# Two gate-and-up pieces of a feed-forward taken as one pair, 512 columns wide

## The chip, the cores and the metric

The kernel runs on one core of a Trainium2 chip. The metric is the device time of one execution in microseconds. Three runs of the kernel before took 752.0, 753.22 and 754.83 us; the median is 753.22.

## The reference

A trunk of two layers over 256 tokens of width 1024: dilated attention, a SwiGLU feed-forward, forgetting attention, a second feed-forward, a last norm. The change lies in the two feed-forwards:

```python
def rmsnorm(x, g):
    xf = x.astype(jnp.float32)
    y = xf * lax.rsqrt(jnp.mean(xf * xf, axis=-1, keepdims=True) + RMS_EPS) * g.astype(jnp.float32)
    return y.astype(x.dtype)

def swiglu(h, w_gu, w_down):
    gu = h @ w_gu
    g, u = gu[..., :D_FF], gu[..., D_FF:]
    return (jax.nn.silu(g) * u) @ w_down
...
        h = h + swiglu(rmsnorm(h, ffn_norm[i]), ffn_w_gu[i], ffn_w_down[i])
```

D_FF is 2816, that is 22 slices of 128.

## The kernel before

**Precision.** Every float32 operand is split into a high and a low part (`split`, L71): ScalarE copies it to the high tile, rounded (L74), VectorE subtracts that from the source into the low tile (L78). A product is then three matrix products, high by high (L197), high by low and low by high (L202), in `mm3`. With `narrow`, `mm3` issues each of the last two as two halves of the columns.

**Weights.** They are streamed through the chip once. `piece` (L85) loads 2048 columns in two transfers of 128 x 1024 into `raw` (five buffers, queue of SP) and splits each half into `wh` and `wl` (four buffers each). `order` lists all pieces in the order in which they go through these buffers; `weights(nm, i)` sees to it that the pieces up to two places behind the wanted one are issued, and hands the wanted one out. In a feed-forward the list is gu0, gu1, gu2, dn0, gu3, gu4, dn1, gu5, gu6, dn2 and so on, so that the fifth piece takes the buffer that the first gives up.

A gate-and-up piece gu*f* holds slice *f* of the gate and slice *f* of the up projection, 128 columns each, for all eight depth blocks of 128.

**The normalised rows.** `xt` holds the normalised activations, features on partitions, high and low. The first token half (t = 0, 128 tokens) is there when the feed-forward starts; the second is made during its first products by `norm_t(*hs[1], grow, xt, 1)`: a scale on VectorE (L185, `xn`), eight transposes on TensorE (L190) into two `tr` banks, and the split from there into `xt`.

**Two forms of a gate-and-up product.** `up(f)` has the weights as the stationary operand and both token halves as 256 moving columns; its result has features on partitions, as the down projection needs it. It wants both token halves. `proj_tok` (L215) has one token half of `xt` as the stationary operand and the piece's 256 columns moving; its result has tokens on partitions and must be transposed afterwards, but one token half is enough. So the first three pieces of each feed-forward, the head, go through `proj_tok`, first for the first token half, all three, with `norm_t` of the second half hooked in at the third depth block of gu2, then for the second half. After that half of a piece `gated` (L674) takes Silu on ScalarE (L677) and the product on VectorE (L678) for both halves at once; two transposes (L730) and a split into `acts` follow. Down projections (`down`) take two slices at a time: down(0) needs slices 0 and 1, down(1) slices 2 and 3.

**The pair.** `proj_pair` (L225) is there before, for value projections of both attentions. It takes two pieces that were laid out so that each holds 512 columns of half of the depth: four depth blocks per piece. Its products move 512 columns. At the last depth block of t = 1 it is narrow.

**Buffers in PSUM.** Eight banks in four tags of two: `mm`, `tr`, `sc`, `o`. The head's three pieces use two of one tag and one of another, `o, o, mm` in the first feed-forward and `mm, mm, o` in the second. down(0) takes both `sc` and both `o`, `up` one `mm` and one `tr`.

**Order.** Tile's scheduler puts the instructions of each engine in order of priority and of their place in the program; `first()` raises the priority, `tc.issue_after` ties it to an instruction. Each engine works through its own queue in that order.

Of the kernel before, what the change touches and what calls it, by code (L numbers as in the profile page):

```python
# [16 lines left out]
P = 128  # L17
D = 1024
S = 256
KT = D // P  # L20
# [4 lines left out]
NF = DFF // P  # L25
# [6 lines left out]
def trunk(ctx: ExitStack, tc: tile.TileContext, T, out):  # L32
# [14 lines left out]
    def psum(tag):  # L47
        return ps.tile([P, 512], F32, tag=tag, name=f"ps_{tag}", bufs=2)
# [88 lines left out]
    for l in range(2):  # L137
        if l == 1:
            order += [("b_in", hq * 3 + w) for hq, w in b_units]
            order += [("b_out", i) for i in range(4)]  # L140
        for f in range(NF):
            order += [(f"gu{l}", f)] + ([(f"dn{l}", f // 2 - 1)] if f % 2 == 0 and f else [])
        order += [(f"dn{l}", NJ - 1)]
    AHEAD = 2
    ready = {}
# [2 lines left out]
    def weights(nm, i, after=None, ahead=AHEAD):  # L148

        upto = order.index((nm, i)) + ahead  # L150
        while state["next"] <= min(upto, len(order) - 1):
            key = order[state["next"]]
            cuts = []
            ready[key] = piece(key, cuts)
            for cut in cuts:
                cut(after)
            state["next"] += 1
        return ready.pop((nm, i))
# [506 lines left out]
    def ffn(l, hs, xt, grow, mid):  # L665
# [3 lines left out]
        def act(f):  # L669
            if f % 2 == 0:  # L670
                acts[f // 2] = tuple(p_tile(512, F32R, f"a{y}") for y in "hl")
            return acts[f // 2], lambda y: y[:, (f % 2) * S:(f % 2 + 1) * S]
# [42 lines left out]


        dn = {}
        head = []
        for f in range(3):
            head.append((weights(f"gu{l}", f), psum((("o", "o", "mm"), ("mm", "mm", "o"))[l][f])))  # L720
            proj_tok(xt, head[f][0], head[f][1][:, :S], 0,
                     hook=(2, lambda: norm_t(*hs[1], grow, xt, 1)) if f == 2 else None)
        for f in range(3):
            o = head[f][1]
            proj_tok(xt, head[f][0], o[:, S:], 1)
            ov = o.rearrange("p (a c b) -> p a c b", a=2, c=2)
            a = gated(ov[:, :, 0, :], ov[:, :, 1, :], 2)
            tr = psum("tr")
            for t in range(2):
                nc.tensor.transpose(tr[:, t * P:(t + 1) * P], a[:, t, :], ident)  # L730
            split(*act(f), tr[:, :S])
        for f in range(2, NF):
            if f > 2:
                up(f)
            if f % 2 == 0:
                j = f // 2 - 1
                dn[j] = weights(f"dn{l}", j)
                down(j, 0, narrow=j >= LATE)
                if j < LATE:
                    down(j, 1, narrow=True)  # L740
# [271 lines left out]
def _layout(i):  # L1012

    perm, t = _constants()
    x = np.asarray(i["x"])[0]
    t["x"] = x
    x_fm = x[perm].T.reshape(KT, P, S)
    t["norms"] = np.stack([np.asarray(i["a_norm"])[0], np.asarray(i["ffn_norm"])[0], np.asarray(i["b_norm"])[0],
                           np.asarray(i["ffn_norm"])[1], np.asarray(i["final_norm"])])
    kmaj = lambda w: w.reshape(KT, P, -1).transpose(1, 0, 2)  # L1020
    a = np.asarray(i["a_w_in"])[0].reshape(KT, P, NG, 3, 4, 256)
    a = np.ascontiguousarray(a.transpose(4, 2, 3, 1, 0, 5))

    v = np.stack([a[:, 1, 2], a[:, 2, 2]], 3).reshape(4, P, 2, 2048)
    a[:, 1:, 2] = v.transpose(0, 2, 1, 3).reshape(4, 2, P, KT, 256)

    def quarters(y):

        y = np.stack([y[:, 0], y[:, 1]], 3)
        return y.reshape(-1, P, 2, 4, 512).transpose(0, 2, 1, 3, 4).reshape(-1, 2, P, KT, 256)  # L1030

    a[:2, 0, 2] = quarters(a[None, :2, 0, 2])[0]
    t["a_in"] = a.reshape(36, P, 2048)

    lead = np.concatenate([x_fm, v[0].reshape(P, KT, 512).transpose(1, 0, 2)], 2)
    t["lead0"] = np.concatenate([lead[0], np.asarray(i["a_norm"])[0].reshape(KT, P).T], 1)
    t["lead1"] = lead[1]
    t["lead"] = lead[2:].reshape(3, 2, P, -1).transpose(0, 2, 1, 3).reshape(3, P, -1)
    b = np.asarray(i["b_w_in"])[0]
    y = np.ascontiguousarray(b[:, :3 * D].reshape(KT, P, 3, 4, 256).transpose(3, 2, 1, 0, 4))  # L1040
    y[:2, 2] = quarters(y[None, :2, 2])[0]
    t["b_in"] = y.reshape(12, P, 2048)
    t["b_f_in"] = kmaj(b[:, 3 * D:]).reshape(P, KT * NH)
    t["bf"] = np.asarray(i["b_f"])[0]
    rows = lambda w: w.reshape(-1, 2, P, D).transpose(0, 2, 1, 3).reshape(-1, P, 2048)
    t["a_out"], t["b_out"] = rows(np.asarray(i["a_w_out"])[0]), rows(np.asarray(i["b_w_out"])[0])
    for l in range(2):
        g = np.asarray(i["ffn_w_gu"])[l].reshape(KT, P, 2, NF, P)
        t[f"gu{l}"] = g.transpose(3, 1, 0, 2, 4).reshape(NF, P, 2048)
        t[f"dn{l}"] = rows(np.asarray(i["ffn_w_down"])[l])  # L1050
    return {k: np.ascontiguousarray(v) for k, v in t.items()}

# [15 lines left out]
```

## Time and profile before

| | |
|---|---|
| median of three runs | 753.22 us (752.0 to 754.83) |
| the profiled execution | 753.38 us, of which the span takes 751.6 |
| instructions | 14534 |
| TensorE | 6008 products |
| head, up(3) and down(0) of the first feed-forward | 266.45 to 296.33 us of the span |
| the same in the second | 561.49 to 591.37 us |

In the profile PE is TensorE's products and PEld its weight loads, which overlap them; DVE is VectorE, ACT ScalarE, POOL GpSimd, SP the queue that issues transfers. L202 is line 202. Products are pipelined: the lengths that the timeline gives for them overlap, and what a product costs is the distance from its start to the start of the next. A wait is shown in square brackets with the work that ended it. Windows give the busy time and the instructions of each engine in a stretch that the reader chooses.

### The profile page before, as it was taken

The numbers are of one execution on the slowest core, as the hardware profiler recorded it, in microseconds if no ns is written. First come the engines' busy times: TensorE is split into PE (matmuls) and PEld (weight loads), VectorE is DVE, ScalarE is ACT, GpSimd is POOL, SyncE is SP. The second block draws the span as 40 slices with busy tenths as digits, with TensorE's granted clock in tenths as the row PEclk, the third lists the DMA queues.
The fourth block names the chain that finished last, engine by engine and source line by source line (L and its number), as shares of the span: only waits on it lengthen the run. The fifth ranks groups of instructions, "written<-read, shape, count | busy, mean of one in ns | idle before, by whom it ended". The sixth has DMA issues, their size and how long they took to land.

```text
span 751.6 us, 14534 instructions
## 1 busy us (share of the span) xinstructions
PE 742.2 (99%) x6008; PEld 683.4 (91%) x6008; DVE 498.5 (66%) x758; ACT 374.8 (50%) x620; POOL 63.8 (8%) x98
## 2 busy tenths in 40 slices
PE   9999999999999999999999999999999999999996
PEld 7998989999988799999999988999789999999995
DVE  6987987877888376454556465798766545456533
ACT  7635527347336455444445355387555444445521
POOL 0600003004003000000000004311000000000000
PEclk9999999999999999999999999999999999999999
DMA  8954553654645267656567433795336665656601
GB/s 329 303 196 170 169 169 124 204 185 136 197 152 186 85 224 236 208 176 205 186 193 255 167 128 128 236 305 183 120 102 220 226 206 174 204 188 214 206 2 56
DMA packets 39586, 138.08 MB, mean 184 GB/s; under 512 B 4544, under 2 KB 5984, under 8 KB 39520
## 3 DMA queue, kind: packets, MB, share of 16 engines
q1 hardware_dynamic: 39376, 137.06, 54.9%
q8 instruction: 47, 0.77, 0.4%
q14 instruction: 19, 0.16, 0.1%
q10 hardware_dynamic: 144, 0.10, 0.0%
HBM read 136.07 MB, written 1.07 MB: 182 GB/s over the span
## 4 chain that ended last, share of the span: by engine, by line
PE 90%; DMA 3%; issue 2%; ACT 2%; DVE 1%; SPq 0%; POOL 0%; POOLq 0%; DVEq 0%; ACTq 0%
PE ps_mm L202 31%; PE ps_mm L197 16%; PE ps_tr L202 9%; PE ps_sc L202 8%; PE ps_o L202 7%; PE ps_tr L197 5%; PE ps_sc L197 4%; PE ps_o L197 3%; PE ps_o L304 2%; PE ps_tr L293 2%; ACT wh L74 1%; DMA otl<-in_lead 1%; DMA raw<-in_b_in 1%; PE ps_sc L450 1%; PE ps_sc L835 1%
## 5 line engine op out<-in xcount | busy, mean ns | idle before, releaser
L74 ACT ACTIVATE wh<-raw 128x1024 fp32r<-128x1024 f32 x236 | 243.7, 1055 | 244.8 <-PE ps_mm L202 81.2
L78 DVE TENSOR_TENSOR wl<-raw,wh 128x1024 fp32r<-128x1024 f32 x236 | 285.5, 1230 | 86.9 <-ACT wh L74 86.7
L197 PE MATMUL ps_mm<-xt,wh 128*128 128x256 f32 x816 | 228.2, 280 | 0.6 <-DVE qk L434 0.6
L202 PE MATMUL ps_mm<-xt,wl 128*128 128x256 f32 x816 | 226.2, 277 | 0.1
L202 PE MATMUL ps_mm<-xt,wh 128*128 128x256 f32 x816 | 226.0, 277 | 0.0
L197 PEld LDWEIGHTS ps_mm<-xt,wh 128*128 128x128 f32 x816 | 153.4, 188 | 4.3 <-issue 3.3
L202 PEld LDWEIGHTS ps_mm<-xt,wl 128*128 128x128 f32 x816 | 153.5, 188 | 0.5 <-DVE wl L78 0.5
L202 PEld LDWEIGHTS ps_mm<-xt,wh 128*128 128x128 f32 x816 | 153.4, 188 | 0.0
L202 PE MATMUL ps_tr<-xt,wl 128*128 128x256 f32 x304 | 83.8, 276 | 0.0
L202 PE MATMUL ps_tr<-xt,wh 128*128 128x256 f32 x304 | 83.8, 276 | 0.0
L197 PE MATMUL ps_tr<-xt,wh 128*128 128x256 f32 x304 | 83.6, 276 | 0.0
L693 DVE TENSOR_TENSOR sa<-ps_tr,sa 128x256 f32<-128x256 f32 x38 | 16.1, 424 | 74.7 <-PE ps_tr L202 74.7
L202 PEld LDWEIGHTS ps_tr<-xt,wh 128*128 128x128 f32 x304 | 57.1, 188 | 0.0
L202 PEld LDWEIGHTS ps_tr<-xt,wl 128*128 128x128 f32 x304 | 57.1, 188 | 0.0
L197 PEld LDWEIGHTS ps_tr<-xt,wh 128*128 128x128 f32 x304 | 56.9, 188 | 0.0
L197 PE MATMUL ps_mm<-wh,xt 128*128 128x256 f32 (+1 forms) x160 | 53.0, 331 | 0.0
L202 PE MATMUL ps_mm<-wh,xt 128*128 128x256 f32 (+1 forms) x164 | 51.9, 320 | 0.0
L202 PE MATMUL ps_mm<-wl,xt 128*128 128x256 f32 (+1 forms) x164 | 51.8, 320 | 0.0
L279 POOL COPY v<-v 32x256 f32<-32x256 f32 x64 | 33.2, 518 | 180.4 <-ACT v L275 177.7
L167 POOL TENSOR_SCALAR rs<-ssq 128x1 f32<-128x1 f32 x7 | 2.2, 319 | 430.3 <-ACT junk L176 430.3
L202 PEld LDWEIGHTS ps_mm<-wl,xt 128*128 128x128 f32 x164 | 30.8, 188 | 2.6
L202 PEld LDWEIGHTS ps_mm<-wh,xt 128*128 128x128 f32 x164 | 30.5, 188 | 2.6
(218 smaller groups left out, 1140.5 us busy)
## 6 DMA issues: line engine op xcount, KB each, us to landing
raw<-in_gu SPq DMA_DIRECT2D x88, 512.0 KB, 4.5
raw<-in_a_in SPq DMA_DIRECT2D x68, 512.0 KB, 4.4
raw<-in_dn SPq DMA_DIRECT2D x44, 512.0 KB, 4.2
raw<-in_b_in SPq DMA_DIRECT2D x24, 512.0 KB, 5.0
raw<-in_a_out SPq DMA_DIRECT2D x8, 512.0 KB, 5.2
raw<-in_b_out SPq DMA_DIRECT2D x8, 512.0 KB, 5.0
bias<-sums SPq DMA_DIRECT2D x8, 384.0 KB, 6.2
grow<-in_norms SPq DMA_DIRECT2D x4, 512.0 KB, 5.1
```

What stands on the lines that cost most here:

```text
L74: a = nc.scalar.activation(view(hi), src, AF.Copy)
L78: return nc.vector.tensor_tensor(view(lo), src, view(hi).bitcast(F32), op=ALU.subtract)
L167: nc.gpsimd.tensor_scalar(m, s, rest, None, op0=ALU.add)
L197: nc.tensor.matmul(o, sh, mh, start=start, stop=False)
L202: last = nc.tensor.matmul(o[:, u], s, m[:, u], start=False, stop=end and u.stop == n)
L279: nc.gpsimd.tensor_copy(v[1 + a % 2][n:n + 32, a // 2 * S:a // 2 * S + S], by_t[a * 32:a * 32 + 32, t, g])
L293: nc.tensor.transpose(tr[:, i * P:(i + 1) * P], b, ident)
L304: nc.tensor.matmul(o[h * HD:(h + 1) * HD], v[:, c:c + HD], w(h), start=start, stop=stop)
L450: nc.tensor.matmul(scs[h][:, qb * P:qb * P + (qb + 1) * P], q[hr[h], pr, qb * P:(qb + 1) * P], k[hr[h], pr, :(qb + 1) * P], start=True, st ...
L693: nc.vector.tensor_tensor(a, u, sg, op=ALU.mult)
L835: last = nc.tensor.matmul(scs[h][:, qb * P:qb * P + (qb + 1) * P], b[0][own[h], pr, qb * P:(qb + 1) * P], b[1][own[h], pr, :(qb + 1) * P], ...
```

## The change

The first two pieces are laid out as a pair: in memory gu0 now holds the first half of the depth of slices 0 and 1, side by side, 512 columns, and gu1 the second half. The head becomes:

1. `proj_pair` with both, first token half; Silu and product of both slices for that half (`gate(0)`).
2. The third piece, first token half, with `norm_t` of the second half hooked in as before.
3. `proj_pair`, second token half; `gate(1)`.
4. The third piece, second token half.
5. The four transposes of slices 0 and 1 into one `tr` bank, and one split of 512 columns into `acts[0]`.
6. `up(3)`; then the third piece's gate, its two transposes and its split; then down(0) and the loop as before.

Before, `up(3)` came behind down(0). In the list of pieces gu3 and dn0 change places, nothing else does. The arithmetic is the same.

```diff
-            order += [(f"gu{l}", f)] + ([(f"dn{l}", f // 2 - 1)] if f % 2 == 0 and f else [])
+            order += [(f"gu{l}", f)] + ([(f"dn{l}", max(f // 2 - 1, 0))] if f == 3 or f % 2 == 0 and f > 3 else [])
...
-        head = []
-        for f in range(3):
-            head.append((weights(f"gu{l}", f), psum((("o", "o", "mm"), ("mm", "mm", "o"))[l][f])))
-            proj_tok(xt, head[f][0], head[f][1][:, :S], 0,
-                     hook=(2, lambda: norm_t(*hs[1], grow, xt, 1)) if f == 2 else None)
-        for f in range(3):
-            o = head[f][1]
-            proj_tok(xt, head[f][0], o[:, S:], 1)
-            ov = o.rearrange("p (a c b) -> p a c b", a=2, c=2)
-            a = gated(ov[:, :, 0, :], ov[:, :, 1, :], 2)
-            tr = psum("tr")
-            for t in range(2):
-                nc.tensor.transpose(tr[:, t * P:(t + 1) * P], a[:, t, :], ident)
-            split(*act(f), tr[:, :S])
+        ws = [weights(f"gu{l}", f) for f in range(2)]
+        pair = [psum(("o", "mm")[l]) for _ in range(2)]
+        rows = {}
+
+        def gate(t):
+            gu = pair[t].rearrange("p (a c b) -> p a c b", a=2, c=2)
+            rows[t] = gated(gu[:, :, 0, :], gu[:, :, 1, :], 2)
+
+        for half in range(2):
+            proj_pair(xt, ws[half], pair, half, (0,))
+        gate(0)
+        wt, o = weights(f"gu{l}", 2), psum(("mm", "o")[l])
+        proj_tok(xt, wt, o[:, :S], 0, hook=(2, lambda: norm_t(*hs[1], grow, xt, 1)))
+        for half in range(2):
+            proj_pair(xt, ws[half], pair, half, (1,))
+        gate(1)
+        proj_tok(xt, wt, o[:, S:], 1)
+        tr = psum("tr")
+        for f in range(2):
             for t in range(2):
-                nc.tensor.transpose(tr[:, t * P:(t + 1) * P], a[:, t, :], ident)
-            split(*act(f), tr[:, :S])
+                nc.tensor.transpose(tr[:, f * S + t * P:f * S + (t + 1) * P], rows[t][:, f, :], ident)
+        act(0)
+        split(acts[0], lambda y: y, tr)
+        third = act(2)
+        up(3)
+        gu = o.rearrange("p (a c b) -> p a c b", a=2, c=2)
+        a = gated(gu[:, :, 0, :], gu[:, :, 1, :], 2)
+        tr = psum("tr")
+        for t in range(2):
+            nc.tensor.transpose(tr[:, t * P:(t + 1) * P], a[:, t, :], ident)
+        split(*third, tr[:, :S])
         for f in range(2, NF):
-            if f > 2:
+            if f > 3:
                 up(f)
...
         g = np.asarray(i["ffn_w_gu"])[l].reshape(KT, P, 2, NF, P)
-        t[f"gu{l}"] = g.transpose(3, 1, 0, 2, 4).reshape(NF, P, 2048)
+        g = g.transpose(3, 1, 0, 2, 4).reshape(NF, P, KT, 256)
+        t[f"gu{l}"] = np.concatenate([quarters(g[None, :2])[0].reshape(2, P, 2048), g[2:].reshape(-1, P, 2048)])
```

What this does to the queues, in the first feed-forward. First TensorE, before, where the head's transposes stand: in the third piece's second token half (`ps_mm_3332`), each group of two for one slice (`sa_3402` and `sa_3436` are the gated slices 0 and 1).

```order
L202 MATMUL ps_mm_3332<-wh_3252,xt_3037 128x256
L730 MATMUL ps_tr_3405<-ident_216,sa_3402 128x128 x2
L197 MATMUL ps_mm_3332<-wh_3252,xt_3037 128x256
L730 MATMUL ps_tr_3439<-ident_216,sa_3436 128x128 x2
L202 MATMUL ps_mm_3332<-wl_3253,xt_3037 128x256
```

The same now, where the third piece's second half ends and `up(3)` begins (`xt` as the moving operand marks it):

```order
L202 MATMUL ps_mm<-wl,xt 128x256
L202 MATMUL ps_mm<-wh,xt 128x256
L738 MATMUL ps_tr<-ident,sa 128x128 x4
L197 MATMUL ps_mm<-xt,wh 128x256
L202 MATMUL ps_mm<-xt,wh 128x256
L202 MATMUL ps_mm<-xt,wl 128x256
```

The four stand in one group, 24 products later relative to the second gate, with `up(3)` behind them instead of down(0). Second, VectorE around the split of the normalised second half (`xt` from `ps_tr`). Before, where `wh_3287` is dn0, `wh_3322` gu3:

```order
L185 SCALAR_TENSOR_TENSOR xn_3343<-h_a_out1_3236,rs_3339,grow_2995 128x512 x2
L78 TENSOR_TENSOR wl_3288<-raw_3291,wh_3287 128x1024
L78 TENSOR_TENSOR xt_3037<-ps_tr_3346,xt_3037 128x4x128
L78 TENSOR_TENSOR xt_3037<-ps_tr_3353,xt_3037 128x4x128
L78 TENSOR_TENSOR wl_3323<-raw_3324,wh_3322 128x1024
L78 TENSOR_TENSOR wl_3323<-raw_3326,wh_3322 128x1024
L678 TENSOR_TENSOR sa_3402<-ps_o_3262,sa_3402 128x256
L678 TENSOR_TENSOR sa_3436<-ps_o_3297,sa_3436 128x256
```

Now, where `wh_3262` is gu3, `wh_3301` dn0, `wh_3421` gu4, and `sa_3298` and `sa_3383` are the gated rows of the first and second token half:

```order
L185 SCALAR_TENSOR_TENSOR xn_3322<-h_a_out1_3236,rs_3318,grow_2995 128x512 x2
L78 TENSOR_TENSOR wl_3263<-raw_3266,wh_3262 128x1024
L678 TENSOR_TENSOR sa_3298<-ps_o_3272,sa_3298 128x256
L78 TENSOR_TENSOR xt_3037<-ps_tr_3325,xt_3037 128x4x128
L78 TENSOR_TENSOR xt_3037<-ps_tr_3332,xt_3037 128x4x128
L78 TENSOR_TENSOR wl_3302<-raw_3303,wh_3301 128x1024
L78 TENSOR_TENSOR wl_3302<-raw_3305,wh_3301 128x1024
L678 TENSOR_TENSOR sa_3383<-ps_o_3273,sa_3383 128x256
L78 TENSOR_TENSOR wl_3422<-raw_3423,wh_3421 128x1024
```

The first gate's product has moved ahead of the split of `xt`, and gu3 and dn0 have changed places. ScalarE's queue shows the same: the load of Silu's table and the first gate's Silu now stand ahead of its two copies to `xt`, and the third gate's Silu stands behind `up(3)`'s. On SP's queue gu0 to gu3 go out as eight transfers in a row, then dn0's two.

## The prediction

> **What bounds the kernel now.** I read the first page, then the engines' busy time by stretches of the span (windows), then the timeline of TensorE, VectorE and ScalarE over the head of the first feed-forward. The page first:
>
> ```profile
> span 751.6 us, 14534 instructions
> PE 742.2 (99%) x6008; PEld 683.4 (91%) x6008; DVE 498.5 (66%) x758; ACT 374.8 (50%) x620; POOL 63.8 (8%) x98
> PEclk9999999999999999999999999999999999999999
> ```
>
> TensorE is busy for 742.2 of 751.6 us at the full granted clock. Of the 9.4 us without it, nearly all lies at the two ends, as the windows show (columns: length; busy us and instructions of PE, PEld, DVE, ACT, POOL; clock; DMA share; GB/s):
>
> ```profile
> 0.00:30.00 30.00, 28.45 (x162) 24.31 (x162) 23.00 (x35) 21.80 (x35) 5.13 (x14) 1.00 0.90 320
> 735.00:752.00 17.00, 9.37 (x48) 7.80 (x46) 7.34 (x17) 3.27 (x10) 1.58 (x4) 0.93 0.17 62
> 266.45:296.33 29.88, 29.82 (x234) 28.45 (x232) 19.87 (x25) 15.67 (x25) 1.80 (x2) 1.00 0.70 234
> ```
>
> The ends hold 1.55 + 7.63 = 9.2 us of it (the last row's 17.00 reaches 0.4 us past the span). The third row is the stretch that the change rewrites in the first layer: from the first product of the feed-forward to the end of its up(3). TensorE idles there for 0.06 of 29.88 us, and the second layer repeats it. So a term counts only if it shortens what TensorE itself does, or takes away what stretches it between two products; what VectorE and ScalarE do counts only where TensorE would wait for it.
>
> **The width.** The first two pieces, each in turn over a token half, fill these four stretches of 48 products of 256 columns; the fifth row is the forgetting attention's pair of pieces, 24 units of 512 columns from the same helper, with the token half as weights too and with the same two narrow splits at its end; the last is up(3), 48 products of 256 columns with wh as weights:
>
> ```profile
> 266.45:272.11 5.66, 5.66 (x50) 5.65 (x48) 5.20 (x7) 3.33 (x7) 1.80 (x2) 1.00 0.70 248
> 275.81:281.46 5.65, 5.65 (x50) 5.65 (x49) 1.48 (x2) 2.56 (x3) 0.00 (x0) 1.00 0.51 170
> 561.49:567.15 5.66, 5.66 (x50) 5.65 (x48) 5.19 (x7) 3.33 (x7) 1.81 (x2) 1.00 0.71 231
> 570.84:576.50 5.66, 5.66 (x50) 5.66 (x49) 1.48 (x2) 2.56 (x3) 0.00 (x0) 1.00 0.44 177
> 462.56:468.07 5.51, 5.51 (x28) 4.60 (x27) 2.01 (x10) 4.29 (x5) 2.91 (x1) 1.00 0.00 0
> 290.87:296.33 5.46, 5.46 (x51) 5.46 (x49) 2.36 (x2) 2.40 (x3) 0.00 (x0) 1.00 0.88 285
> ```
>
> A product of 256 columns costs 5.66/48 = 118 ns, one of 512 costs 5.51/24 = 230 ns: joining two saves 6 ns, no more. The four stretches sum to 22.63 us, four pairs at 5.51 to 22.04: **0.59 us less in both layers**. From below the bound is nothing (512 columns at twice 118); from above it is the fastest column of the table, up(3)'s, at 24 x 2 x 5.46/48 = 5.46 a pair, 0.79 us for four. I take the pair's row, because it is the same shape with the same roles.
>
> **The transposes.** Now the end of the old head, TensorE's timeline (start, length), and the eight transposes of the normalised rows for the price of a longer group:
>
> ```profile
> 272.82 1.03 PE L190 MATMUL ps_tr<-ident,xn 128*128 128x128 f32 x8
> 273.61 0.36 PE L197 MATMUL ps_mm<-wh,xt 128*128 128x256 f32 x1
> 273.81 0.28 PE L202 MATMUL ps_mm<-wl,xt 128*128 128x256 f32 x1
> ```
>
> ```profile
> 282.76 0.28 PE L202 MATMUL ps_mm<-wh,xt 128*128 128x256 f32 x1
> 283.11 0.44 PE L730 MATMUL ps_tr<-ident,sa 128*128 128x128 f32 x2
> 283.30 0.37 PE L197 MATMUL ps_mm<-wh,xt 128*128 128x256 f32 x1
> 283.50 0.38 PE L730 MATMUL ps_tr<-ident,sa 128*128 128x128 f32 x2
> 283.64 0.36 PE L202 MATMUL ps_mm<-wl,xt 128*128 128x256 f32 x1
> 283.84 0.28 PE L202 MATMUL ps_mm<-wh,xt 128*128 128x256 f32 x1
> ...
> 285.49 0.47 PE L202 MATMUL ps_sc<-wh,al 128*128 128x512 f32 x1
> 285.80 0.40 PE L197 MATMUL ps_sc<-wh,ah 128*128 128x512 f32 x1
> ...
> 286.50 0.38 PE L730 MATMUL ps_tr<-ident,sa 128*128 128x128 f32 x2
> 286.64 0.48 PE L197 MATMUL ps_sc<-wh,ah 128*128 128x512 f32 x1
> 286.96 0.40 PE L202 MATMUL ps_sc<-wl,ah 128*128 128x512 f32 x1
> ```
>
> ```profile
> 281.46:285.02 3.56, 3.50 (x31) 3.29 (x29) 2.81 (x5) 3.55 (x7) 0.00 (x0) 1.00 0.57 201
> 576.50:580.06 3.56, 3.50 (x31) 3.29 (x29) 2.81 (x5) 3.55 (x7) 0.00 (x0) 1.00 0.70 188
> ```
>
> The third piece's second half, 24 products, should take 24 x 118 ns = 2.83 us and takes 3.56 in either layer: 0.73 us go to the four transposes of the first two pieces and the wait ahead of them (the first starts 0.35 us after the product before it, not 0.12). The eight in one group cost 273.81 - 272.82, less one product, 0.87 us; so four cost 0.44. The change gives them one group with nothing to wait for: **0.73 - 0.44 = 0.29 us a layer, 0.58 in both**. Ends: the old wait comes back too (0.23 of the 0.29 are gone), or the group goes in at a little under its share of the eight, 0.39.
>
> The old down(0) came right behind and waited for al: its third product holds the next back for 0.31 us instead of 0.23. With up(3) now between transposes and down(0) this goes: 0.08 a layer, **about 0.15 in both**. The third piece's own two transposes cost 286.96 - 286.50, less one 512-wide product, 0.23 us where they stand; they move behind up(3) and cost that again: nothing.
>
> A rule speaks against the grouping: the Trainium skill, "Perfetto Trace Analysis", Optimizing Scalar/DVE Operations, says that where these engines cause bubbles on others, breaking up instructions may let work finish sooner, and here two copies of 256 columns become one of 512. By it the al wait would grow instead of going; in this trace the bubble is those 0.08 us, and the new order puts the 5.46 us of up(3) over the longer copy, so the sum keeps 0.15.
>
> **What is costed at nothing, and its cover.** ScalarE and VectorE around the first layer's normalisation:
>
> ```profile
> 268.85 1.05 ACT L74 ACTIVATE wh<-raw 128x1024 fp32r<-128x1024 f32 x1
> 273.45 1.09 ACT L74 ACTIVATE xt<-ps_tr 128x512 fp32r<-128x512 f32 x2 [3.56 <-PE ps_tr L190]
> 278.89 2.01 ACT L74 ACTIVATE wh<-raw 128x1024 fp32r<-128x1024 f32 x2 [4.34 <-issue]
> 280.91 1.28 ACT L677 ACT_TABLE_LOAD   x1
> 282.21 0.66 ACT L677 ACTIVATE sa<-ps_o 128x256 f32<-128x256 f32 x2
> ```
>
> ```profile
> 271.51 1.42 DVE L185 SCALAR_TENSOR_TENSOR xn<-h_a_out,rs,grow 128x512 f32<-128x512 f32 x2 [0.47 <-POOL rs L170]
> 272.84 1.22 DVE L78 TENSOR_TENSOR wl<-raw,wh 128x1024 fp32r<-128x1024 f32 x1
> 274.08 1.29 DVE L78 TENSOR_TENSOR xt<-ps_tr,xt 128x512 fp32r<-128x512 f32 x2
> 282.62 0.76 DVE L678 TENSOR_TENSOR sa<-ps_o,sa 128x256 f32<-128x256 f32 x2 [0.29 <-ACT sa L677]
> ```
>
> - *The norm's transposes come earlier.* TensorE reaches them 0.15 us sooner. xn's second half ends at 272.93 and the fifth transpose, at about 272.82 + 0.43 = 273.25, comes down to 273.10: still covered, by 0.17. Without the cover, 0.15 a layer.
> - *The first gate stands ahead of the norm's split on ScalarE and VectorE.* The new pair's first half ends at 266.45 + 5.51, some 272.1 with the pipeline's tail; its Silu falls into ScalarE's idle 3.56 us, which hold the table load too, and its product goes behind the wl that ends at 274.06. It pushes xt's low half back by about 0.4: first half done at 274.06 + 0.41 + 0.68 = 275.15. TensorE wants it at the third product of the second token half, 275.66 + 2 x 0.23 = 276.12. Spare: 0.97 us.
> - *Pieces 3 and dn0 change places* in SP's queue and in the ring of four buffers. gu3 takes dn0's old place (cut at 268.85, done by 274.06, wanted after 284). dn0 takes gu0's buffer, free when the pair's first depth half is through, so about where gu3 was cut, 278.9 to 282; wanted at down(0), by the sum below about 290. Spare: 8 us; if it went, every us late would be paid once.
> - *The third gate waits on ScalarE behind up(3)'s own Silu*; the third transposes come 5.46 us of products later, the gate takes 0.4 and 0.4. Behind it gu5's cut waits for up(3) to end, and two copies to act buffers queue behind that; down(1) wants them 11 us later (down(0) and up(4)).
>
> The sum: 0.59 + 0.58 + 0.15 = 1.3 us. The profiled execution took 753.38 us (span 751.6), 0.16 above the median of the three runs, 753.22. So 752.1 for such an execution, and **751.9 us** against the median. TensorE hardly waits between the heads and the end, so I let the gain through whole. 0.5% is 3.8 us; about that much a measurement of this kernel can tell from no change.
>
> **Rivals.**
> *Width gives nothing*: a 512-wide product costs twice a 256-wide. Then 0.73 us remain, 752.5. The pair's row in this very trace speaks against it; the different sources (two pieces, depth halves) leave a little. Chance 0.08.
>
> *Slower: the gate holds up VectorE.* If the first gate's product lands late by more than the 0.97 us spare, TensorE stands still before the second token half, in both layers. The price beyond it is one for one; with one more pair of wl cuts of 2 x 1.22 in front of it, 2.44 - 0.97 = 1.47 a layer, less 0.66 gained: +1.6, so 754.8. It eats the gain from 1.63 us of lateness on and shows as over 0.5% slower only from about 3.5. The Silu would be ready at 272.5, or 273.8 if the table load only went after the wait; the wl ahead ends at 274.06 in any case. Chance 0.05.
>
> *Faster: the weight loads pace TensorE.* PEld is busy through all of the 256-wide stretches (5.65 of 5.66), and the change drops 92 of its loads (46 a layer, the narrow splits taken off). Were the load the bound, a stretch would halve: four times 2.83, 11.3 us, 741.9. But the 512-wide row has PEld busy for 4.60 of 5.51 only and still takes 230 ns a product: TensorE is bound by columns. Chance 0.02.
>
> The Trainium skill, "TensorE: Matmul & The Clock Gate", Back-to-back issue gap, has a sustained spacing of 81 ns at 128 columns and 131 ns at 512 for streams of load and product. With 98 between them for 256, an estimate from that page, a join would save 65 ns and the change 6 us, about 746.5 with the other terms. The trace does not agree: 118 and 230 ns.
>
> **How the numbers follow.** The forecast has 0.80; 0.05 is left for what the runs' own scatter does. With the terms at their ends the gain goes from 0 + 0.12 + 0.0 - 0.3 to 0.79 + 0.68 + 0.15: 753.4 to 751.6. The three runs lie from 1.2 below to 1.6 above their median, and a median of a few may move by half to all of that: the range is 750.4 to 754.0, with rival one inside it, and most of rival two and all of three outside. Faster by over 0.5% (under 749.5) needs rival three or scatter: 0.05. Slower by over 0.5% (above 757.0) needs a far worse rival two: 0.03. Within: 0.92.
>
> **What would show it.** Right: the pair's stretches take 5.5 us instead of 5.66, the four transposes one group of 0.44 without idle time, no wait at down(0), and the stretch from the first product to the end of up(3) and down(0) is 29.2 us instead of 29.88 in either layer; DMA and TensorE elsewhere unchanged. Wrong: idle time of TensorE ahead of the pair's second half or of the norm's transposes, or a 512-wide product at other than 230 ns, or a stretch behind the head that grows by what the head gave.

## The result, and the profile after

The changed kernel takes 751.29 us (median of 22 runs, 749.86 to 754.94) where the kernel before takes 753.39 (22 runs, 750.76 to 757.84): a ratio of 0.9972, 95% interval 0.9959 to 0.9985, so 2.1 us less, between 1.1 and 3.1. The forecast was 751.9, a gain of 1.3. The page of the profiled execution after:

```profile
span 748.3 us, 14346 instructions
PE 739.2 (99%) x5916; PEld 677.7 (91%) x5916; DVE 498.1 (67%) x756; ACT 375.2 (50%) x618; POOL 64.2 (9%) x98
```

There are 92 products fewer, as said, and the span is 3.3 us shorter. Not all of that is the change. Ahead of the first head the program's order is the old one. The windows of before, up to the first head, between the heads, and the second head:

```profile
0.00:266.45 266.45, 264.65 (x2466) 239.28 (x2467) 211.18 (x340) 139.46 (x227) 35.34 (x74) 1.00 0.56 187
296.33:561.49 265.16, 264.94 (x1952) 242.90 (x1951) 166.88 (x265) 137.81 (x248) 23.22 (x16) 1.00 0.56 185
561.49:591.33 29.84, 29.78 (x233) 28.44 (x232) 19.87 (x25) 15.67 (x25) 1.81 (x2) 1.00 0.71 231
```

(In the second layer up(4) begins at 591.33; the table of before, which ends that stretch at 591.37, puts it 0.04 too long.) The same three of after:

```profile
0.00:264.70 264.70, 262.99 (x2466) 237.97 (x2467) 211.16 (x340) 139.38 (x227) 35.57 (x74) 1.00 0.56 188
293.77:558.93 265.16, 264.98 (x1953) 242.93 (x1951) 165.97 (x263) 137.60 (x247) 23.40 (x16) 1.00 0.56 184
558.93:588.01 29.08, 29.08 (x187) 26.24 (x186) 20.48 (x26) 16.11 (x25) 1.81 (x2) 1.00 0.75 243
```

The same 2466 products ahead of the head took 1.75 us less in the one execution: that is the scatter of executions. Between the heads both stand at 265.16. What the change did is in the heads, 29.84 to 29.08 in the second layer, and in the first layer by parts (after):

```profile
264.70:270.19 5.49, 5.49 (x25) 4.51 (x24) 5.03 (x7) 4.72 (x8) 1.80 (x2) 1.00 0.70 240
270.19:273.91 3.72, 3.72 (x34) 3.69 (x33) 3.65 (x6) 1.47 (x3) 0.00 (x0) 1.00 0.73 236
273.91:279.41 5.50, 5.50 (x29) 4.58 (x27) 1.41 (x2) 2.01 (x2) 0.00 (x0) 1.00 0.57 214
279.41:282.49 3.08, 3.08 (x30) 3.08 (x29) 2.80 (x4) 2.44 (x4) 0.00 (x0) 1.00 0.69 197
282.49:288.05 5.56, 5.56 (x52) 5.56 (x51) 4.14 (x5) 3.00 (x5) 0.00 (x0) 1.00 0.90 287
288.05:293.77 5.72, 5.72 (x30) 4.81 (x29) 3.45 (x5) 2.59 (x4) 0.00 (x0) 1.00 0.77 268
264.70:293.77 29.07, 29.07 (x187) 26.23 (x186) 20.48 (x26) 16.23 (x25) 1.80 (x2) 1.00 0.73 244
```

The two rows of before that the prediction did not show, the third piece's first half and down(0) with the third transposes:

```profile
272.11:275.81 3.70, 3.70 (x34) 3.70 (x33) 3.24 (x5) 1.09 (x2) 0.00 (x0) 1.00 0.90 271
285.02:290.87 5.85, 5.85 (x31) 4.70 (x29) 4.78 (x8) 2.75 (x5) 0.00 (x0) 1.00 0.68 230
```

| first layer, us | before | after | difference |
|---|---|---|---|
| pair, first and second token half | 5.66 + 5.65 | 5.49 + 5.50 | -0.32 |
| third piece, first half, with the norm's transposes | 3.70 | 3.72 | +0.02 |
| third piece, second half, with the transposes of slices 0 and 1 | 3.56 | 3.08 | -0.48 |
| up(3) | 5.46 | 5.56 | +0.10 |
| down(0) and the third transposes | 5.85 | 5.72 | -0.13 |
| head | 29.88 | 29.07 | -0.81 |

So the heads give 0.81 + 0.76 = 1.57 us, inside the measured interval; 1.3 was forecast. (In the second layer the old down(0) with the third transposes took 5.81 us, not 5.85.) One thing was not foreseen. TensorE's timeline after, from the pair's narrow end to up(3):

```profile
278.96 0.39 PE L202 MATMUL ps_o<-wl,xt 128*128 128x256 f32 x2
279.18 0.39 PE L202 MATMUL ps_o<-wh,xt 128*128 128x256 f32 x2
279.41 0.28 PE L197 MATMUL ps_mm<-wh,xt 128*128 128x256 f32 x1
279.52 0.28 PE L202 MATMUL ps_mm<-wl,xt 128*128 128x256 f32 x1
...
282.13 0.60 PE L738 MATMUL ps_tr<-ident,sa 128*128 128x128 f32 x4
282.49 0.36 PE L197 MATMUL ps_mm<-xt,wh 128*128 128x256 f32 x1
282.69 0.28 PE L202 MATMUL ps_mm<-xt,wh 128*128 128x256 f32 x1
```

The 24 products from 279.41 to 282.13 take 2.72 us, 113.3 ns each, where the same products with the same operands took 118 everywhere in the old head. The four transposes cost 282.69 - 282.13 less a product of 0.11, 0.45 us, and nothing waits ahead of them.

### The profile page after: what moved, and what is told of

Its sections match the earlier page's. It is cut to its first block, busy times and chain, and to the rows that moved or that the text cites. A ratio compares the mean times of both kernels' runs of the same rounds, so it can differ in the third digit from the quotient of the medians.

```text
span 748.3 us, 14346 instructions
## 1 busy us (share of the span) xinstructions
PE 739.2 (99%) x5916; PEld 677.7 (91%) x5916; DVE 498.1 (67%) x756; ACT 375.2 (50%) x618; POOL 64.2 (9%) x98
## 4 chain that ended last, share of the span: by engine, by line
PE 92%; DMA 3%; ACT 2%; DVE 1%; issue 1%; SPq 0%; POOL 0%; POOLq 0%; DVEq 0%; ACTq 0%
PE ps_mm L202 31%; PE ps_mm L197 16%; PE ps_tr L202 9%; PE ps_sc L202 8%; PE ps_o L202 7%; PE ps_tr L197 5%; PE ps_sc L197 4%; PE ps_o L197 4%; PE ps_o L304 2%; PE ps_tr L293 2%; DMA raw<-in_b_in 1%; PE ps_sc L450 1%; DMA otl<-in_lead 1%; PE ps_sc L852 1%; PE ps_sc L466 1%
## 5 line engine op out<-in xcount | busy, mean ns | idle before, releaser
L197 PE MATMUL ps_mm<-wh,xt 128*128 128x512 f32 (+1 forms) x144 | 50.1, 348 | 0.0
L202 PE MATMUL ps_mm<-wh,xt 128*128 128x512 f32 (+1 forms) x149 | 49.2, 336 | 0.0
L202 PE MATMUL ps_mm<-wl,xt 128*128 128x512 f32 (+1 forms) x149 | 49.1, 335 | 0.0
L197 PE MATMUL ps_sc<-wh,ah 128*128 128x512 f32 x80 | 31.4, 392 | 0.0
L202 PE MATMUL ps_sc<-wl,ah 128*128 128x512 f32 (+1 forms) x82 | 31.3, 385 | 0.0
```

Of the source, the lines that this page charges most:

```text
L197: nc.tensor.matmul(o, sh, mh, start=start, stop=False)
L202: last = nc.tensor.matmul(o[:, u], s, m[:, u], start=False, stop=end and u.stop == n)
```

## The experiments

All heads below run from the first product of the feed-forward to the first of up(4) and are read within one execution. All but e_mixed ran once, and single totals cannot judge them: the kernel before alone spread over 7 us. The waits of TensorE show some of where that comes from. The waits of e_pair (experiment 4) and of e_place (experiment 8) each have one far from the head, 2.0 and 2.7 us (0.2 us before and after):

```profile
PE ps_sc L849 <- DVE p L855: 2.0, 1, 2.0
```

and of e_place:

```profile
PE ps_sc L836 <- DVE p L842: 2.7, 1, 2.7
```

The theory behind the first four (theory A): a product of 256 columns has two spacings, 118 and 113 ns; a run keeps the one that it starts with, and a block with a *narrow* end (its two corrections in halves) makes the run behind it short-spaced.

**1. The pair without its narrow end** (e_wide_end).

```diff
...
-            proj_pair(xt, ws[half], pair, half, (1,))
+            proj_pair(xt, ws[half], pair, half, (1,), narrow=())
```

> After without the narrow end of the pair in the feed-forward: the last depth block's two correction products stay 512 wide. Both kernels are read by the head's length, first product of the feed-forward to the first of up(4): 29.88 us before, 29.07 after. Theory A (a run of products keeps the spacing it starts with, 118 ns at 256 columns, and a narrow end lets it fall to 113): the third piece's second half goes back from 2.72 to 2.83 us, the head to 29.18. Rival B (the third piece is faster in the new kernel because VectorE and ScalarE or the DMA leave the memory alone there, or because of its place): it stays at 2.72 and the head at 29.07.

```profile
264.79:294.13 29.34, 29.34 (x186) 26.45 (x184) 20.47 (x26) 16.22 (x25) 1.80 (x2) 1.00 0.75 241
279.48:282.31 2.83, 2.83 (x25) 2.83 (x24) 2.56 (x4) 2.28 (x3) 0.00 (x0) 1.00 0.63 194
282.67:288.40 5.73, 5.73 (x51) 5.73 (x49) 4.03 (x5) 2.99 (x5) 0.00 (x0) 1.00 0.89 282
```

The third piece's second half is back at 2.83 in the same place, with the same work beside it: rival B is out. The head is longer than expected, 29.34, because up(3), behind the four transposes, stays long-spaced too: 5.73 instead of 5.56. The kernel with the narrow end is 0.27 us a layer shorter than the one without, a third of the 0.81. That the narrow end alone does it is not shown: the end of experiment 9 has what speaks against it.

**2. A narrow end in the old kernel** (e_lead), in `out_proj`:

```diff
-                           both(ws[k // 2], ALL, slice(c, c + 512)), k == 0, k == KT - 1)
+                           both(ws[k // 2], ALL, slice(c, c + 512)), k == 0, k == KT - 1,
+                           t == 1 and n == 1 and k == KT - 1)
```

> The old kernel with one thing added: the last depth block of the output projection ahead of the head ends in narrow products (two of 256 columns for one of 512). Theory A (spacing is a state that a narrow end resets): the 54 products of 256 columns up to the normalisation's transposes fall from 118 to about 113.3 ns, the first stretch of 48 from 5.66 to 5.45 us; after the eight transposes they are at 118 again, so the head is about 29.63 us instead of 29.88. Then the gain from the pair's width is no fixed price for each product, as the prediction had it, but the cost of a state that 256 columns can leave as well. Rival B (118 ns is the price of 256 columns with xt as weights, whatever went before): 5.66 and 29.88 stay.

```profile
265.48:295.15 29.67, 29.61 (x234) 28.19 (x233) 19.75 (x25) 15.65 (x25) 1.78 (x2) 1.00 0.71 233
265.48:270.92 5.44, 5.44 (x51) 5.44 (x50) 4.98 (x7) 3.30 (x7) 1.78 (x2) 1.00 0.65 209
```

As theory A has it: 5.44 us, and in the second layer too. Nothing of the change is in this kernel, and its first stretch is shorter than the pair's 5.49. Two products of 256 columns at 113.3 ns, 226.6, cost less than one of 512 at 229. The Trainium skill, "Perfetto Trace Analysis", Optimizing Tensor Performance, says that larger matmuls are more efficient than smaller ones; here that holds against 118 ns and not against 113.3.

**3. The order without the width** (e_order): the old pieces and layout, then the new order of transposes, up(3) and down(0). Against after:

```diff
-        for half in range(2):
-            proj_pair(xt, ws[half], pair, half, (0,))
-        gate(0)
...
+        for f in range(3):
+            o = head[f][1]
+            proj_tok(xt, head[f][0], o[:, S:], 1)
+            if f < 2:
+                ov = o.rearrange("p (a c b) -> p a c b", a=2, c=2)
+                rows[f] = gated(ov[:, :, 0, :], ov[:, :, 1, :], 2)
...
```

> After without the width: the first two pieces one at a time at 256 columns as before, in the old layout, but their four transposes in one group behind the third piece, up(3) ahead of down(0), the loads in the new order. The prediction's terms: transposes 0.29 and the al wait 0.08 a layer, so a head of 29.88 - 0.37 = 29.51 us, the four stretches still 5.66. Theory A says the same, since no narrow end stands ahead of the third piece: its second half 2.83 us. Rival B (the third piece is faster by its place): 2.72 and a head of 29.40. Rival C (the group gains nothing without the earlier gates): 29.8.

```profile
265.13:294.79 29.66, 29.66 (x234) 28.75 (x232) 20.56 (x26) 15.88 (x25) 1.80 (x2) 1.00 0.71 236
283.32:289.06 5.74, 5.74 (x52) 5.74 (x50) 4.76 (x6) 3.15 (x6) 0.00 (x0) 1.00 0.80 256
```

The gain is 0.22 a layer, not 0.37. What is missing is again up(3): no narrow end stands ahead of it any more (before, down(0) ended narrow right ahead of it), and it takes 5.74, where after's takes 5.56. Against e_wide_end, which also has no narrow end ahead of up(3), this kernel lacks the width alone (and gates by piece instead of by token half); its head is 29.66 where that one's is 29.34, so the width gives 0.32.

**4. The width without the order** (e_pair): the pair, then down(0) straight behind the head, and up(3) behind that.

```diff
...
-        third = act(2)
-        up(3)
...
-            if f > 3:
+            if f > 2:
```

> After with the width alone: the pair side by side, but down(0) straight behind the head and up(3) behind that, loads in the old order, the copies to the activation buffers one for each piece. The transposes of the pair still stand in one run of four, since both gates are done by then. The prediction's terms: width 0.29 and transposes 0.29 a layer without the 0.08 of the al wait: a head of 29.30 us, or 29.19 with the third piece's second half at 2.72 (theory A). Rival C (down(0) now waits longer, since the copies have only up(3)'s first products as cover): TensorE idles ahead of down(0) and the head is 29.5 or more.

```profile
264.18:293.53 29.35, 29.35 (x187) 26.17 (x186) 19.69 (x25) 15.87 (x25) 1.80 (x2) 1.00 0.72 236
281.97:288.41 6.44, 6.44 (x34) 5.19 (x33) 4.46 (x7) 2.95 (x6) 0.00 (x0) 1.00 0.94 296
```

The head is 0.53 shorter than before's. The pair's halves are 5.50 and the third piece's second half 2.73, as in after; the 0.28 us that it lacks lie where up(3) and down(0) are, 11.56 us together (281.97 to 293.53) against 5.56 + 5.72 in after. The program's order is not quite the old one there: three products of up(3) stand ahead of down(0), and the third transposes in its midst. The 0.53 here and the 0.22 of experiment 3 can't be added to the 0.81, since both kernels have the four transposes in one group. A row in which each step adds one thing is before 29.88, e_order 29.66, e_wide_end 29.34, after 29.07: the order with the grouped transposes gives 0.22, the width 0.32, and the step to the narrow end 0.27.

**5. VectorE made late** (e_gate_late), for the rival in which the first gate holds up TensorE.

```diff
+                    for _ in range(times - 1):
+                        nc.vector.tensor_tensor(view(lo), src, view(hi).bitcast(F32), op=ALU.subtract)
                     return nc.vector.tensor_tensor(view(lo), src, view(hi).bitcast(F32), op=ALU.subtract)
...
-        proj_tok(xt, wt, o[:, :S], 0, hook=(2, lambda: norm_t(*hs[1], grow, xt, 1)))
+        proj_tok(xt, wt, o[:, :S], 0, hook=(2, lambda: norm_t(*hs[1], grow, xt, 1, (4, 2)[l])))
```

> After with VectorE made late on the path of the gate and the normalisation's split: the low half of the normalised rows' first four blocks is written again, 3 times more in the first layer (one of them behind the other half's), once more in the second, 0.65 us each. It tests the spare time that the prediction put at 0.97 us. Spare as said (and as after's rows give it, 1.1): no wait in the second layer; in the first the last write comes 2.6 us later and TensorE stands for about 1.4 to 1.6 us ahead of the pair's second half, a head of about 30.5 us. Rival (TensorE isn't held by this write): 29.07 in both. Rival (the spare time is under 0.65): a wait in the second layer too.

Both heads, and the product that waited in the first:

```profile
265.92:296.50 30.58, 29.65 (x187) 26.61 (x186) 22.41 (x29) 16.22 (x25) 1.80 (x2) 1.00 0.70 231
562.44:591.83 29.39, 29.39 (x187) 26.54 (x186) 21.04 (x27) 16.12 (x25) 1.81 (x2) 1.00 0.74 241
```

```profile
277.16 0.50 PE L204 MATMUL ps_o<-wh,xt 128*128 128x512 f32 x1 [0.93 <-DVE xt L80]
```

One more write costs no wait, three more hold TensorE: the spare time is over 0.65 us and under about 2.6. Of the 1.51 us by which the first head is longer than after's, 0.93 is idle time of TensorE, where a wait of 1.4 to 1.6 was expected. That the head still came out near the expected 30.5 is luck: its third piece and up(3) lost their short spacing too, some 0.28 us. The second head is 29.39 without any wait, for the same loss; in this kernel two products of the third piece stand between those of the pair. In after itself the order of VectorE answers to the prediction's list:

```profile
272.22 0.42 DVE L678 TENSOR_TENSOR sa<-ps_o,sa 128x256 f32<-128x256 f32 x1
272.56 1.28 DVE L78 TENSOR_TENSOR xt<-ps_tr,xt 128x512 fp32r<-128x512 f32 x2
```

The low half's first part, 0.68 us long, is done at 272.56 + 0.68 = 273.24, wanted at 273.91 + 2 x 0.23 = 274.37: spare 1.13, where 0.97 was said.

**6. More narrow ends, for a faster version.** e_256_narrow takes e_order and puts a narrow block at the output projection's end and at the third piece's first block behind the norm's transposes:

```diff
...
+                     narrow=(2,) if f == 2 else ())
```

> No pair at all: the first two pieces one at a time at 256 columns in the old layout, the new order of transposes, up(3) and down(0), and two narrow ends in each layer: at the output projection's last block, and at the first block of the third piece behind the normalisation's transposes (halves of 128 columns there). Theory A: all 256-wide products but the first few behind the transposes run at 113.3 ns, so the four stretches are 5.44 each, the third piece's second half 2.72, and the head 29.66 (the same order without narrow ends) less 0.25, 0.40 and 0.17 for up(3), about 28.84 us: shorter than the pair's 29.07, so the width is not what the gain comes from. Rival (halves of 128 columns reset nothing, or joining two products still saves a price of its own): the second stretch stays at 5.66 and the head is 29.3 or longer.

```profile
265.29:294.98 29.69, 29.69 (x236) 28.70 (x235) 20.45 (x26) 15.98 (x25) 1.78 (x2) 1.00 0.73 237
274.68:280.33 5.65, 5.65 (x50) 5.65 (x49) 1.48 (x2) 2.56 (x3) 0.00 (x0) 1.00 0.50 190
```

e_pair_narrow takes after and adds narrow blocks at the output projection's end, at the pair's first half, and in the third piece's first half:

```diff
...
-            proj_pair(xt, ws[half], pair, half, (0,))
+            proj_pair(xt, ws[half], pair, half, (0,), narrow=(0,))
...
+                 narrow=((2,), (KT - 1,))[l])
```

> After with more narrow ends: at the output projection's last block, at the pair's first token half, and in the third piece's first token half, in the first layer at the first block behind the normalisation's transposes, in the second layer at its last block. Theory A, with 226.7 ns for 512 columns in the short-spaced state (the output projection's rows) instead of 229: the pair's halves 5.44 instead of 5.50, the third piece's first half 0.04 and in the first layer another 0.07 shorter: heads of 28.86 and 28.93 us instead of 29.07. Rival (512 columns take 229 ns with xt as weights whatever goes before): only the third piece gains, heads of 28.96 and 29.03.

```profile
264.72:294.29 29.57, 29.57 (x192) 26.86 (x191) 20.45 (x26) 16.20 (x25) 1.78 (x2) 1.00 0.70 240
560.31:589.91 29.60, 29.60 (x193) 26.87 (x192) 20.46 (x26) 16.18 (x25) 1.79 (x2) 1.00 0.74 237
```

Both miss. Behind the halves of 128 columns the second stretch stays at 5.65, and with blocks added the later one at the pair's end no longer worked: either head of e_pair_narrow is half a microsecond longer than after's. Theory A, that a narrow end always makes the next run short-spaced, falls. Five more kernels asked what does.

**7. What of the narrow block does it** (e_lead_how): the old kernel with two other forms at the place of experiment 2.

```diff
+        if narrow == "alternate":
+            for c in (0, n // 2):
+                u = slice(c, c + n // 2)
+                nc.tensor.matmul(o[:, u], sh, ml[:, u], start=False, stop=False)
+                last = nc.tensor.matmul(o[:, u], sl, mh[:, u], start=False, stop=stop and u.stop == n)
+            return last
         for s, m, end in ((sh, ml, False), (sl, mh, stop)):
+            cut = narrow if narrow != "last" else s is sl
...
```

> The old kernel again with an end at the output projection, in two other forms, one for each layer. First layer: the last block's two corrections in halves of 256 columns, but the weights alternate from product to product (high, low, high, low). Second layer: only the very last product is split, in two with the same weights. The full form (both corrections split, each weight twice in a row) gave 5.44 us for the next 48 products of 256 columns, where 5.66 stood. Theory A1 (short products alone reset the spacing): 5.44 in both layers. Theory A2 (it takes the same weights twice in a row, by which a load comes free): 5.66 in the first layer, 5.44 in the second. Theory A3 (it takes four short products): 5.44 in the first, 5.66 in the second.

```profile
265.70:271.14 5.44, 5.44 (x50) 5.44 (x49) 4.98 (x7) 3.31 (x7) 1.78 (x2) 1.00 0.68 230
560.74:566.39 5.65, 5.65 (x50) 5.65 (x49) 5.18 (x7) 3.43 (x7) 1.80 (x2) 1.00 0.77 229
```

At this place, in one layer each, four short products did it and two did not; the order of their weights made no difference (A3).

**8. How many blocks, and where** (e_count, e_place): still the old kernel.

```diff
...
+                           t == 1 and k >= KT - 2 and n >= {"a_out": 1, "b_out": 0}[nm])
```

> The old kernel with more narrow blocks at the output projection's end: the last two blocks in the first layer (four products more between the normalisation's transposes and the head), the last four in the second (eight more). So far one narrow block, two products more, went with short spacing behind it (5.44 us for 48 products, 113.3 ns each), and none or one more with long spacing (5.66, 118 ns). Theory A (a narrow end resets the spacing, however often): 5.44 in both layers. Theory D (what counts is the number of products since the transposes, taken three at a time: short spacing where it is two more than a multiple of three, as 14, 26 and 44 were, long where it is not, as 12, 13, 36, 40 and 46 were): 16 in the first layer, so 5.66; 20 in the second, so 5.44.

```profile
266.38:272.04 5.66, 5.66 (x50) 5.66 (x49) 5.20 (x7) 3.40 (x7) 1.75 (x2) 1.00 0.74 222
563.84:569.49 5.65, 5.65 (x51) 5.65 (x50) 5.18 (x8) 3.24 (x6) 1.71 (x2) 1.00 0.74 244
```

```diff
...
+                           t == 1 and (n, k) in {"a_out": [(0, 7), (1, 6), (1, 7)], "b_out": [(1, 6)]}[nm])
```

> The old kernel once more with narrow blocks in the output projection's end: in the first layer the last three blocks, in the second a single one, but a block earlier than before, with three whole products of 512 columns behind it. So far one block at the very end gave short spacing to the next 48 products of 256 columns (5.44 us), two and four gave long (5.66). Theory E (each narrow block turns the state over, an odd number leaves it short, wherever they stand): 5.44 in both layers. Theory F (one block alone, straight ahead of the 256-wide run, and nothing else): 5.66 in both. Theory G (one block alone does it, but its place doesn't matter): 5.66 in the first, 5.44 in the second.

```profile
266.61:272.26 5.65, 5.65 (x50) 5.65 (x49) 5.19 (x8) 3.36 (x7) 1.72 (x2) 1.00 0.72 223
565.73:571.38 5.65, 5.65 (x49) 5.65 (x48) 5.18 (x7) 3.29 (x7) 1.77 (x2) 1.00 0.71 231
```

Two, three and four blocks do not do it, nor one with three whole products behind it. Theories A, D, E and G fall; F stands for this place: one block alone, straight ahead.

**9. An earlier block beside the pair's own** (e_mixed, e_pick). e_mixed, the candidate for a faster version, has the first half in 256 columns behind a narrow block:

```diff
...
-        for half in range(2):
-            proj_pair(xt, ws[half], pair, half, (0,))
+        for f in range(2):
+            for k in range(KT):
+                st = both(xt, ALL, k, ALL)
+                c = k % 4 * 512 + f * 256
+                mm3(pair[0][:, f * 256:(f + 1) * 256], [x[:, :P] for x in st],
+                    both(ws[k // 4], ALL, slice(c, c + 256)), k == 0, k == KT - 1)
```

> After, with the pair's first token half piece by piece in products of 256 columns again (the pair's layout kept) and one narrow block at the output projection's end; the second token half side by side with its narrow end as in after. Theory A and theory D both: the first half 5.44 us and the next six products 0.68 at 113.3 ns, instead of 5.49 and 0.72; the second half and everything behind it as in after: a head of about 28.98 us instead of 29.07, so 256 columns at a time in the short-spaced state beat the pair. Rival (the narrow end of the second half only helps if the first half was wide): the third piece's second half and up(3) at 118 ns, a head of about 29.25.

```profile
266.30:295.65 29.35, 29.35 (x213) 27.45 (x211) 20.46 (x26) 16.11 (x25) 1.78 (x2) 1.00 0.72 241
266.30:271.74 5.44, 5.44 (x50) 5.44 (x49) 4.98 (x7) 4.59 (x8) 1.78 (x2) 1.00 0.68 236
281.00:283.83 2.83, 2.83 (x27) 2.83 (x26) 2.54 (x4) 2.28 (x3) 0.00 (x0) 1.00 0.54 179
```

The first half is 5.44, but the third piece's second half is long-spaced again. It took 752.35 us (10 runs) against 753.6 (13): ratio 0.998, 0.9955 to 1.0004. No version here has shorter heads than the changed kernel in both layers. e_pick has after with one block more, at the output projection's end in the first layer, at the pair's first half in the second:

```diff
...
+                           nm == "a_out" and t == 1 and n == 1 and k == KT - 1)
...
+            proj_pair(xt, ws[half], pair, half, (0,), narrow=((), (0,))[l])
```

> After with one narrow block more, in the first layer at the output projection's end ahead of the pair, in the second at the end of the pair's first token half. Where both stood (and two more in the third piece's first half in all), and where the first half was in products of 256 columns behind such a block, the block at the end of the pair's second half no longer left short spacing. Theory H (one block earlier in the layer is enough to undo the later one): the third piece's second half 2.83 us and up(3) at 118 ns in both layers, heads of about 29.3 us instead of 29.07. Rival (the later block works as in after, since the normalisation's transposes lie between): 2.72 and 29.07 or a little under in both. If the layers differ, the place of the earlier block decides.

```profile
267.47:296.52 29.05, 29.05 (x188) 26.21 (x187) 20.46 (x26) 16.10 (x25) 1.78 (x2) 1.00 0.71 242
562.86:592.23 29.37, 29.37 (x189) 26.64 (x188) 20.48 (x26) 16.22 (x25) 1.81 (x2) 1.00 0.73 243
```

The layers differ: the block at the output projection's end leaves the later one its effect, the one at the pair's first half takes it. In e_mixed the block stands where it stands in e_pick's first layer, and the later effect is gone. So neither place nor number alone decides.

The traces hold a sign that none of these kernels was built to test. In the pair's second half one product of each depth block is short: 226 ns to the next start, where the other two take 229 and 232 (read to the nanosecond, block after block). In after, e_pair and the first layer of e_pick it is the second of the three. There the narrow end's own products stand 113 to 114 ns apart, and the third piece goes on at 113.3. In e_mixed, e_pair_narrow and e_gate_late it is the third, in the second layer of e_pick the first. There the narrow end's products stand 117 to 120 ns apart, and the third piece goes on at 118. All fourteen traces agree, the pairs of the two attentions included: 41 narrow ends behind a short second product had this short spacing in their own products, and 44 behind another order had the long one.

So the narrow end takes up a spacing that is there before it. And e_wide_end differs from after before the edit: up to the narrow end of the first layer both give TensorE the same products in the same order, yet in e_wide_end, in both layers, the short product is the third. No narrow end behind that order was followed by a short-spaced run, so experiment 1 can't tell what the narrow end itself is worth; a wide end behind after's order was not run. What sets this order, and with it the spacing of a run, stays open.

## Why the prediction was right, and where it was short

- *TensorE is the bound; only what shortens its own work counts.* Held: the head has no idle time after, and between the heads both kernels take 265.16.
- *Width, 0.59 in both layers.* Measured 0.32 a layer, 0.65 in both with the second layer's 5.49 and 5.50; experiments 1 and 3, which differ in the width alone, give 0.32 again. The size was right, the reason only in part. "Joining two saves 6 ns, no more" is true of 118 ns products; experiment 2 shows that the old ones could have run at 113.3, and then joining loses about 2.4.
- *Transposes, 0.58.* Third piece's second half and up(3) together went from 9.02 to 8.64, 0.38 a layer. 24 x 4.7 ns = 0.11 of that is spacing, so 0.27 is the group, as against 0.29 forecast, with 0.45 for the four (0.44 forecast).
- *The al wait, 0.08 a layer.* down(0) with the third transposes gave 0.13, in the second layer 0.08 (5.81 to 5.73). The third product of down(0) no longer stretches, as the rows of after show: 288.97 - 288.74 = 0.23.

```profile
288.74 0.40 PE L202 MATMUL ps_sc<-wh,al 128*128 128x512 f32 x1
288.97 0.39 PE L197 MATMUL ps_sc<-wh,ah 128*128 128x512 f32 x1
```

  The third transposes' own price moved with it; the two were not told apart.
- *Moved at no cost.* No wait of TensorE lies in either head: the gate, the norm's transposes, the swap of gu3 and dn0 and the third gate were covered as said.
- *The step that was short:* "the third piece's second half, 24 products, should take 24 x 118 ns = 2.83 us". It takes 2.72. And up(3) was carried over at its old price, 5.46, without a word on what makes it cheap. It pays 5.56 behind the transposes; 0.09 of the added 0.10 is its first product, 0.20 us long and part of the group's 0.45. In experiment 1 it pays 5.73. Both hang on the one thing that the prediction had in its rows (118 in the head, 113.8 in up(3)) and took for roles of operands. It counted for 0.11 us a layer of what was missed. That up(3) kept its price was luck: the 0.17 us a layer more of experiment 1 could as well have come.
- *The rivals.* Width gives nothing: out, by 5.49. The gate holds up VectorE: real as a mechanism from somewhere between 0.65 and 2.6 us of lateness (experiment 5), but with 1.13 spare it did not come. Weight loads pace TensorE: out, PEld is busy 4.51 of the pair's 5.49 us. The Trainium skill, "TensorE: Matmul & The Clock Gate", Back-to-back issue gap, has 131 ns a product at 512 columns; 229 were measured.
- The heads account for 1.6 of the measured 2.1 us. The interval, 1.1 to 3.1, holds 1.6, so there may be nothing more; no run here places the other 0.5.

## What to carry to other kernels

Read the price of a product from rows in the place where it will stand, and expect that it may have two: the same product cost 118 or 113 ns here, and that was worth 0.27 us a layer where the width gave 0.32. Judge changes of a microsecond in 750 by the length of the changed stretch within one execution, and the total only by many runs. When parts of a change are moved together, build kernels that differ by one step each, and look at the stretch ahead of the edit too: here before, e_order, e_wide_end and after make such a row, and the last step turned out not to be a clean one.

## What was not expected of the hardware

- Products of 256 columns have two spacings, 113.3 and 118 ns, at a granted clock of 1.00 in both, with the same operands. A run of 54 kept one of them throughout; up(3) in after starts at 117 to 123 behind the transposes and is at 113.3 from its sixth product on.
- The order of the program alone does not fix the spacing. Well ahead of the heads before and after have the same 144 products of 256 columns in the same place, behind the same narrow end. Before, then after:

```profile
179.19:196.15 16.96, 16.96 (x146) 16.96 (x145) 12.40 (x16) 7.45 (x9) 6.85 (x13) 1.00 0.54 182
178.27:194.61 16.34, 16.34 (x147) 16.34 (x145) 12.45 (x16) 7.58 (x9) 7.29 (x13) 1.00 0.55 184
```

  That is 0.62 of the 1.75 us by which the two executions differ ahead of the first head. Here the narrow end was short-spaced before and long-spaced after, and the run behind it the other way round. So it was with all 28 runs of up(3)'s roles (weights stationary) that stand straight behind the narrow end of an attention's pair.
- A single block of four short products straight ahead of the run left it short-spaced, at the place of experiment 2, in seven of seven layers with that block (e_lead, e_256_narrow and e_mixed twice each, e_lead_how once); none, two short products, two to four blocks, or one followed by whole products left it long-spaced.
- The eight transposes of the norm turned a short-spaced run long in each of these. Behind the four transposes of the head up(3) starts long either way; in after it falls back to 113.3, in experiment 1 it stays at 118 (5.56 and 5.73).
